# A hybrid GLA and S5 decoder block: the S5 tables loaded beside the scan and built second matrix first, the powers transposed one product later, two buffers for the attention output

## The chip, the cores and the metric

The kernel runs on one core of a Trainium2 chip. The core has five engines that run their own instruction streams in order: TensorE (PE in the profile, with its weight loads as PEld), VectorE (DVE), ScalarE (ACT), GpSimd (POOL) and SyncE (SP). SP, ACT and POOL also issue DMAs, each in the order of its own queue. The metric is the device time of one execution in microseconds; lower is better.

## The reference

What is computed, cut to what matters here: a GLA attention branch and a grouped complex-diagonal S5 branch on the same projected input, gated and added, then a squared-ReLU MLP.

```python
xn = rmsnorm(h, g_mix_pre[l]);  proj = xn @ w_in[l]      # q, k, v, r, a_low, u, z_gla, z_ssm
log_a = log_sigmoid(a_low @ w_gate_up[l] + b_gate[l]) / GATE_TAU
o = gla_chunked(q * DK**-0.5, k, v, log_a)               # 4 heads, key 128, value 256
o = rmsnorm(o, gla_norm_g[l]) * silu(r);  y_gla = o @ w_o_gla[l]
# S5: 64 groups of 16 channels, 64 complex states each
lam = exp((a_re + 1j * a_im) * dt);  bb = (lam - 1) / (a_re + 1j * a_im) * b
x_t = lam * x_{t-1} + bb @ u_t;      y_t = real(c @ x_t) + d_skip * u_t
glu = gelu(y_s) @ w_glu[l] + b_glu[l];  y_ssm = glu[:D] * sigmoid(glu[D:])
mixed = sigmoid(z_gla) * y_gla + sigmoid(z_ssm) * y_ssm
h = h + rmsnorm(mixed @ w_out[l], g_mix_post[l])
h = h + rmsnorm(square(relu(rmsnorm(h) @ w_ff1[l])) @ w_ff2[l])
```

512 tokens and 16 meta tokens, width 1024, all in float32.

## The kernel before, in words

**Products.** Activations stand with features on the partitions. Each product of 128 output features is one entry of the list `dense` and one call of `slot()`: a weight tile of 128x1024 is loaded by SP (`wraw`, line 167), ScalarE rounds it to its high half (`whi`, L161), VectorE subtracts to get the low half (`wlo`, L176), and PE runs 24 matmuls of 512 columns (eight steps of whi by xh, whi by xl, wlo by xh; `mm3`, L60 in the profile since a helper issues every matmul). Each of the three tiles has three buffers, and a slot fetches two weights ahead, so the halves of the third product on can only be made when a product has ended. The list is in this order: u3 to u7 (S5 input), four z_ssm gates and one z_gla gate, then per head v, v, k, q and a z_ssm gate, then four z_gla gates, r0 to r7 (the gate r of the attention output), and z5, o0, o1, o2, z6, o3, o4, z7, o5, o6, o7, where o is the output projection. PE keeps the order of the program; on VectorE and ScalarE a list scheduler sets the order of the instructions when the program is built, after data and buffers.

**S5.** 64 groups in eight blocks of eight. First come parameters in `chain` and `powers`: Lr and Li are the powers 0 to 8 of lam, E8 those of the normalised lam to the eighth. `lam_rows` transposes Lr and Li on PE (16 transposes of 64x64, line 65), ScalarE copies them to `lamn`, and they are written to DRAM (`lamd`, L776). `b_rows` turns the scaled input matrix (tile `bar`), `c_rows` the output matrix (tiles `cnat` and `cnatx` into CA and CB, L745). Each block then has two matrices, made by `tables` on VectorE in four pieces: the first, M1 (64 complex states by eight steps by 16 channels), from B and lam, which are loaded from DRAM by broadcast (L994, L996); the second, M2, from CA, CB, Lr and Li (L986 to L988). `turns` makes the rotations E of the block (`erot`, L236 to L239), `kernels` the impulse response from M2 (written to `kpad` and read again as M3, L1046), `scan` the states (16 matmuls of U and M1, then v, a scan, X; L1052 to L1069), `output` the result.

**The loop.** One iteration per block b has five slots. Between them stand the attention of head b (`decays`, `turn_values`, `turn_keys`, `scores`, `states`), the outputs of head b-1, and the S5 work: turns(b), the loads of block b+1, a slot, kernels(b) and output(b-1), a slot, scan(b), and then the four pieces of the tables of block b+1, one after each of the scan and the next slots. B and lam have one buffer each, and M1's pieces work on B in place.

**Attention outputs.** `outputs` ends with `on` (L960), `turn_outputs` transposes its two halves into PSUM, ScalarE scales each into `oT` (L969), and GpSimd's queue stores it (`og`, L970). A product r later reads it back (`ro`), and VectorE multiplies (L1120, L1121) and splits it (`ogl`, L1123). The four PSUM banks named `sm` serve all such transposes in rotation.

The lines that the change and the prediction's steps touch:

Of the kernel before, what the change touches and what calls it, by code (L numbers as in the profile page):

```python
# [12 lines left out]
ALU = mybir.AluOpType  # L13
# [3 lines left out]
P = 128  # L17
D = 1024
KT = D // P
SEQ = 512  # L20
# [16 lines left out]
T8 = 8  # L37
NCK = NT // T8
NST = NCK - 1
GRP = 64  # L40
NST_N = 64
HG = 16
GB = 8
NBLK = GRP // GB
# [5 lines left out]
def hybrid_block(ctx: ExitStack, tc: tile.TileContext, io, out: bass.AP):  # L50
    nc = tc.nc
    V, S, G = nc.vector, nc.scalar, nc.gpsimd
# [267 lines left out]
    V, S = InOrder(nc.vector), InOrder(nc.scalar)  # L320
# [107 lines left out]
    V, S = nc.vector, nc.scalar  # L428
# [122 lines left out]
    CA = mk(p5, [P, GRP, HG], tag="CA")  # L551
# [249 lines left out]
        pass  # L801
    slot()
    powers()
    lam_rows()
    b_rows()
    slot()
    for s_ in cr:
        pass
    sga.close()
    st5.close()  # L810

# [7 lines left out]

    kmetas = [mk(pgb, [P, P], tag=f"kmeta{i}") for i in range(2)]  # L820
    vmetas = [mk(pgb, [P, DV], tag=f"vmeta{i}") for i in range(2)]
    for t in (*kmetas, *vmetas):
        G.memset(t, 0.0)

    class Head:
# [136 lines left out]
        def turn_outputs(self):  # L962
            for v in range(2):
                m = 2 * self.h + v
                ps = bank()
                for t in range(TT):
                    PE.transpose(ps[:, t * P : (t + 1) * P], self.on[:, t, v * P : (v + 1) * P], ident)
                oT = mk(pgb, [P, SEQ], tag="oT", bufs=1)
                S.activation(oT, ps, AF.Copy, scale=vecs[:, V_GN + m : V_GN + m + 1])  # L969
                nc.gpsimd.dma_start(og_dram[m], oT)  # L970

    class Block:
# [14 lines left out]
            V.tensor_mul(ta, b_[:, gg].unsqueeze(2).to_broadcast(sh), lib)  # L987
            V.tensor_add(d, d, ta)  # L988

        def loads(self):  # L990

            self.B = mk(b5, [P, GB, 2, NST_N], tag="B")
            self.lam = mk(b5, [P, 2, GB, NST_N], tag="lam")
            nc.sync.dma_start(self.B.rearrange("p g c n -> p (g c n)"), bard[:, self.gs, :].rearrange("h g n -> h (g n)").unsqueeze(0).to_broadcast([T8, HG, GB * 2 * NST_N]))  # L994
            for i in range(2):
                nc.sync.dma_start(self.lam[:, i].rearrange("p g n -> p (g n)"), lamd[i, :, self.gs, :].rearrange("l g n -> l (g n)").unsqueeze(1).to_broadcast([T8, HG, GB * NST_N]))  # L996

        def tables(self):

            M1 = self.M1 = mk(b5, [P, GB, 2, NST_N], tag="M1", bufs=1)  # L1000
            self.M2 = mk(b5, [P, GB, 9, HG], tag="M2", bufs=2)
            B, (lr, li) = self.B, (self.lam[:, i].unsqueeze(2).to_broadcast([P, GB, 2, NST_N]) for i in range(2))
            V.tensor_mul(M1, B, lr)
            yield
            self.table(self.M2, 9, CA, CB, 0)
            yield
            V.tensor_mul(B, B, li)  # L1007
            V.tensor_sub(M1[:, :, 0], M1[:, :, 0], B[:, :, 1])
            V.tensor_add(M1[:, :, 1], M1[:, :, 1], B[:, :, 0])
            yield  # L1010
            self.table(self.M2, 9, CA, CB, 4)
            yield

        def turns(self):

            self.d0 = mk(b5, [P, GB, NST], tag="d0")
            S.copy(self.d0, prm[:, M8, self.gs].unsqueeze(2).to_broadcast([P, GB, NST]))
            G.memset(self.d0[:, :, 0:1], 0.0)
            self.E = mk(b5, [P, 2, GB, NST], tag="E")
            S.copy(self.E[:, :, :, :9], E8[:, :, self.gs, :])  # L1020
            U = self.U = mk(b5, [P, GB, NCK], tag="U", bufs=2)

            for sp in range(T8):
                nc.sync.dma_start(U[sp * HG : (sp + 1) * HG], ud[self.blk][:, :, T8 - 1 - sp, :].rearrange("g h c -> h g c"))
            for n in (8, 16, 32):
                erot(self.E, n, n, b5)
# [14 lines left out]
        def scan(self):  # L1041

            M3 = self.M3 = mk(b5, [P, GB, P], tag="M3", bufs=1)
            for sp in range(T8):
                s = T8 - 1 - sp
                nc.sync.dma_start(M3[sp * HG : (sp + 1) * HG], kpad[self.gs].rearrange("g h l -> h g l")[:, :, 112 - 16 * s : 240 - 16 * s])  # L1046
            U, E = self.U, self.E
            v, vs = (mk(b5, [P, GB, NST], tag=t, bufs=1) for t in ("v", "vs"))

            def turn(src, gg):  # L1050

                V.tensor_mul(vs[:64, gg], src[64:], E[64:, 1, gg])  # L1052
                V.tensor_mul(vs[64:, gg], src[:64], E[:64, 1, gg])  # L1053

            for g0 in range(0, GB, 4):
                ps = bank()
                pv = ps[:, : 4 * NST].rearrange("p (g c) -> p g c", g=4)
                for g in range(4):
                    PE.matmul(pv[:, g], self.M1[:, g0 + g].rearrange("p c n -> p (c n)"), U[:, g0 + g, :NST], start=True, stop=True)
                gg = slice(g0, g0 + 4)  # L1060
                V.tensor_mul(v[:, gg], pv, E[:, 0, gg])
                turn(pv, gg)
            V.tensor_sub(v, v, vs)
            flat = v.rearrange("p g c -> p (g c)")
            V.tensor_tensor_scan(flat, self.d0.rearrange("p g c -> p (g c)"), flat, 0.0, op0=ALU.mult, op1=ALU.add)  # L1065
            X = self.X = mk(b5, [P, GB, NST], tag="X", bufs=1)
            V.tensor_mul(X, v, E[:, 0])
            turn(v, slice(0, GB))
            V.tensor_add(X, X, vs)  # L1069
# [80 lines left out]
    for kind, m in (("z", 5), ("o", 0), ("o", 1), ("o", 2), ("z", 6), ("o", 3), ("o", 4), ("z", 7), ("o", 5), ("o", 6), ("o", 7)):  # L1150
        if kind == "o":
            o_slot(m)
        else:
            gate_slot(C_ZG, m, zg)
    blocks[0].loads()
    first = blocks[0].tables()
    for _ in range(4):
        next(first, None)
# [1 line left out]
    for b, blk in enumerate(blocks):  # L1160
        this = heads[b] if b < HEADS else None
        last = heads[b - 1] if 0 < b <= HEADS else None
        blk.turns()
        following = iter(())
        if b + 1 < NBLK:
            blocks[b + 1].loads()
            following = blocks[b + 1].tables()
        slot()
        blk.kernels()
        if b:  # L1170
            blocks[b - 1].output()
        if this:
            this.decays()
        slot()
        blk.scan()
        if last:
            last.outputs()
        if this:
            this.query_decay()
        next(following, None)  # L1180
        slot()
        if this:
            this.turn_values()
        next(following, None)
        slot()
        if this:
            this.turn_keys()
        if last:
            last.turn_outputs()
        if b == HEADS:  # L1190
            sgb.close()
            sg.close()
            so = ExitStack()
            po_ = pool("po", stack=so, padded=True)
            ogh = mk(po_, [P, KT, SEQ], F32R, tag="ogh")
            ogl = mk(po_, [P, KT, SEQ], F32R, tag="ogl")
        next(following, None)
        slot()
        if this:
            this.scores()  # L1200
            this.states()
        if b:
            blocks[b - 1].turn_output()
        next(following, None)
# [347 lines left out]
```

## Time and profile before

| | |
|---|---|
| median of three runs | 918.82 us (918.14 to 924.5) |
| the profiled execution | 919.62 us, its span 917.9 us |
| granted TensorE clock, mean | 0.989 |
| busy: PE, DVE, ACT, POOL | 889.4, 668.6, 402.4, 91.0 us |
| HBM | 191 GB/s over the span |

How to read it: the span runs from the first to the last instruction of one execution. A timeline row gives start and length in us, engine, line, operation, tile written and tiles read, and in brackets the idle time of the engine ahead of it with what ended it. A row of the waits gives who waited for whom: us in total, times, the longest. A row of the windows gives a stretch, its length, then busy us and number of instructions of PE, PEld, DVE, ACT and POOL, the granted clock, the busy share of the DMA engines and GB/s. A row of groups gives busy us, mean ns, idle time. SPq rows are the issue of a DMA on SP's queue, with waiting for room in it. Rows with a start, a length and no idle bracket that name only engine and line come from the chain that ended last.

### The profile page before, as it was taken

The page shows a single profiled execution, that of the slowest core. Times are in us where ns is not written, and L with a number is a line of the kernel's source. Part 1 is how long each engine was busy: PE and PEld are TensorE (multiplying, and loading weights), DVE is VectorE, ACT ScalarE, POOL GpSimd, SP SyncE. Part 2 cuts the span into 40 slices and gives each one's busy share as a digit, 9 for nine tenths or more (in the row PEclk, how much of TensorE's full clock was granted, in tenths as well). Part 3 has the DMA queues.
Part 4 walks back from the last instruction along what each step waited for, and adds up shares of the span by engine and source line. Part 5 has one row for each costly group of instructions (what it writes and reads, how often), then busy time and mean ns, then how long its engine had stood idle before and what let it go on. Part 6 is the DMA issues. An engine that isn't in the chain of part 4 may idle for free.

```text
span 917.9 us, 13370 instructions
## 1 busy us (share of the span) xinstructions
PE 889.4 (97%) x4924; PEld 755.2 (82%) x4924; DVE 668.6 (73%) x1182; ACT 402.4 (44%) x656; POOL 91.0 (10%) x169
## 2 busy tenths in 40 slices
PE   8998999999999999699999999999999999999996
PEld 6997898889898788588888888988888888888885
DVE  7896968959696879936644566576766668688786
ACT  6362353655653343312433454332332226666663
POOL 1221100010202011021200000011111100000001
PEclk9998999999999999999999999999999999999999
DMA  7745756373746575547854683359898976966664
GB/s 230 204 117 174 173 143 147 82 192 84 184 92 185 130 210 130 150 130 223 279 161 140 178 237 102 138 179 344 291 332 294 347 250 206 302 203 188 182 207 139
DMA packets 175588, 176.13 MB, mean 192 GB/s; under 512 B 22637, under 2 KB 137393, under 8 KB 175522
## 3 DMA queue, kind: packets, MB, share of 16 engines
q1 hardware_dynamic: 159280, 118.94, 47.0%
q0 software_dynamic: 15072, 52.39, 16.4%
q10 hardware_dynamic: 1170, 3.94, 1.2%
q8 instruction: 39, 0.64, 0.3%
q14 instruction: 27, 0.22, 0.1%
HBM read 139.81 MB, written 35.42 MB: 191 GB/s over the span
## 4 chain that ended last, share of the span: by engine, by line
PE 80%; DVE 7%; issue 5%; DMA 4%; ACT 2%; SPq 1%; DVEq 0%; POOL 0%; ACTq 0%; POOLq 0%
PE mm L60 59%; PE sm L60 19%; PE sm L65 2%; DMA wraw<-in_w_in_dram 1%; DMA b<-bd 1%; DMA og<-oT 1%; DVE wlo L176 1%; DMA xt<-in_x_dram 0%; DVE vs L1052 0%; DVE v L1065 0%; PE mm L65 0%; DVE B L1007 0%; SPq L1046 0%; DVE b L484 0%; DVE vs L1053 0%
## 5 line engine op out<-in xcount | busy, mean ns | idle before, releaser
L161 ACT ACTIVATE whi<-wraw 128x1024 fp32r<-128x1024 f32 x101 | 106.8, 1059 | 223.7 <-PE mm L60 196.0
L176 DVE TENSOR_TENSOR wlo<-wraw,whi 128x1024 fp32r<-128x1024 f32 x101 | 123.2, 1221 | 86.6 <-ACT whi L161 86.6
L60 PE MATMUL mm<-xh,whi 128*128 128x512 f32 (+2 forms) x544 | 184.6, 339 | 0.5 <-ACT xh L78 0.5
L60 PE MATMUL mm<-xh,wlo 128*128 128x512 f32 (+2 forms) x544 | 180.8, 332 | 3.7 <-DVE wlo L176 3.6
L60 PE MATMUL mm<-xl,whi 128*128 128x512 f32 (+2 forms) x544 | 180.5, 332 | 0.7 <-DVE xl L78 0.7
L60 PEld LDWEIGHTS mm<-xh,wlo 128*128 128x128 f32 x544 | 104.2, 192 | 13.8 <-DVE wlo L176 4.0
L60 PEld LDWEIGHTS mm<-xh,whi 128*128 128x128 f32 x544 | 104.3, 192 | 11.8 <-issue 1.0
L60 PEld LDWEIGHTS mm<-xl,whi 128*128 128x128 f32 x544 | 104.2, 192 | 9.6 <-DVE xl L78 1.1
L60 PE MATMUL mm<-hh,whi 128*128 128x512 f32 (+1 forms) x280 | 104.0, 371 | 0.0
L60 PE MATMUL mm<-hl,whi 128*128 128x512 f32 (+1 forms) x280 | 103.8, 371 | 0.0
L60 PE MATMUL mm<-hh,wlo 128*128 128x512 f32 (+1 forms) x280 | 103.8, 371 | 0.0
L1429 DVE TENSOR_TENSOR wlo<-wraw,whi 128x1024 fp32r<-128x1024 f32 x56 | 68.4, 1223 | 21.0 <-ACT whi L1425 20.9
L60 PE MATMUL sm<-wlo,fh 128*128 128x512 f32 x192 | 74.8, 390 | 0.0
L60 PE MATMUL sm<-whi,fh 128*128 128x512 f32 x192 | 74.7, 389 | 0.0
L60 PE MATMUL sm<-whi,fl 128*128 128x512 f32 x192 | 74.7, 389 | 0.0
L1425 ACT ACTIVATE whi<-wraw 128x1024 fp32r<-128x1024 f32 x56 | 58.7, 1049 | 18.3 <-PE mm L60 11.7
L60 PEld LDWEIGHTS mm<-hh,whi 128*128 128x128 f32 x280 | 52.8, 188 | 9.1
L60 PEld LDWEIGHTS mm<-hh,wlo 128*128 128x128 f32 x280 | 52.7, 188 | 9.1
L60 PEld LDWEIGHTS mm<-hl,whi 128*128 128x128 f32 x280 | 52.8, 188 | 8.9
L60 PE MATMUL mm<-gh,whi 128*128 128x512 f32 x128 | 49.8, 389 | 0.0
L60 PE MATMUL mm<-gl,whi 128*128 128x512 f32 x128 | 49.8, 389 | 0.0
L60 PE MATMUL mm<-gh,wlo 128*128 128x512 f32 x128 | 49.8, 389 | 0.0
(422 smaller groups left out, 1589.2 us busy)
## 6 DMA issues: line engine op xcount, KB each, us to landing
wraw<-in_w_ff_dram SPq DMA_DIRECT2D x56, 512.0 KB
wraw<-in_w_in_dram SPq DMA_DIRECT2D x48, 512.0 KB
w2raw<-in_w_ff_dram POOLq DMA_DIRECT2D x16, 1024.0 KB, 8.7
t2d<-w2t POOLq DMA_DIRECT2D x16, 1024.0 KB, 5.9
wraw<-t2d SPq DMA_DIRECT2D x32, 512.0 KB
wraw<-in_w_glu_dram SPq DMA_DIRECT2D x16, 512.0 KB
B<-bard SPq DMA_DIRECT2D x8, 512.0 KB
lam<-lamd SPq DMA_DIRECT2D x16, 256.0 KB
```

The source lines that it names most:

```text
L60: ins = nc.tensor.matmul(*args, **kw)
L65: ins = nc.tensor.transpose(*args, **kw)
L161: S.activation(dst, src, AF.Copy, scale=scale)
L176: V.tensor_sub(lo, raw, f32(hi))
L1425: halved = S.activation(bh, raw, AF.Copy)
L1429: V.tensor_sub(bl, raw, f32(bh))
```

## The change

Five edits:

1. `lam_rows()` is called behind the next slot and behind the rest of `c_rows`, not right behind `powers()`.
2. `loads` of block b+1 is called behind `scan(b)`, not behind `turns(b)`. The loads of block 0 are issued by GpSimd's queue, the others by SP's as before.
3. `tables` makes both pieces of M2 first and then both pieces of M1.
4. `oT` has two buffers.
5. `d0`, the factor of the scan, is one tile for all blocks, filled with zeros once; each block's copy writes all but its first column, and the eight small fills of that column are gone.

```diff
@@ preparation
     slot()
     powers()
-    lam_rows()
     b_rows()
     slot()
     for s_ in cr:
         pass
+    lam_rows()
...
-    for t in (*kmetas, *vmetas):
+    d0 = mk(b5, [P, GB, NST], tag="d0")
+    for t in (*kmetas, *vmetas, d0):
         G.memset(t, 0.0)
@@ turn_outputs
-                oT = mk(pgb, [P, SEQ], tag="oT", bufs=1)
+                oT = mk(pgb, [P, SEQ], tag="oT", bufs=2)
@@ loads
-        def loads(self):
+        def loads(self, queue=nc.sync):
...
-            nc.sync.dma_start(self.B...)
+            queue.dma_start(self.B...)
             for i in range(2):
-                nc.sync.dma_start(self.lam...)
+                queue.dma_start(self.lam...)
@@ tables
+            for g0 in (0, 4):
+                self.table(self.M2, 9, CA, CB, g0)
+                yield
             V.tensor_mul(M1, B, lr)
-            yield
-            self.table(self.M2, 9, CA, CB, 0)
             yield
             V.tensor_mul(B, B, li)
             V.tensor_sub(M1[:, :, 0], M1[:, :, 0], B[:, :, 1])
             V.tensor_add(M1[:, :, 1], M1[:, :, 1], B[:, :, 0])
             yield
-            self.table(self.M2, 9, CA, CB, 4)
-            yield
@@ turns
-            self.d0 = mk(b5, [P, GB, NST], tag="d0")
-            S.copy(self.d0, prm[:, M8, self.gs].unsqueeze(2).to_broadcast([P, GB, NST]))
-            G.memset(self.d0[:, :, 0:1], 0.0)
+            S.copy(d0[:, :, 1:], prm[:, M8, self.gs].unsqueeze(2).to_broadcast([P, GB, NST - 1]))
@@ the loop
-    blocks[0].loads()
+    blocks[0].loads(nc.gpsimd)
...
         if b + 1 < NBLK:
-            blocks[b + 1].loads()
             following = blocks[b + 1].tables()
...
         blk.scan()
+        if b + 1 < NBLK:
+            blocks[b + 1].loads()
```

How the order of instructions moves, at three places. First TensorE in the preparation, before. The product of mm_1039 is u7, that of whi_928 the first z_ssm gate; Lr and Li are the powers, bar the B rows:

```order
L60 MATMUL mm_1039<-xh_98,wlo_846 128x272
L65 MATMUL sm_1123<-ident_79,Lr_484 64x64 x8
L65 MATMUL sm_1133<-ident_79,Li_485 64x64 x8
L65 MATMUL sm_1144<-ident_79,bar_522 128x64 x8
L65 MATMUL sm_1154<-ident_79,bar_522 128x64 x8
L60 MATMUL mm_1170<-xh_98,whi_928 128x512
```

And now, where whi_1008 is the second z_ssm gate:

```order
L60 MATMUL mm_1149<-xh_98,wlo_930 128x512
L65 MATMUL sm_1177<-ident_79,cnat_510 128x128 x4
L65 MATMUL sm_1183<-ident_79,cnatx_511 128x128 x4
L65 MATMUL sm_1189<-ident_79,cnat_510 128x128 x4
L65 MATMUL sm_1195<-ident_79,cnatx_511 128x128 x4
L65 MATMUL sm_1201<-ident_79,Lr_484 64x64 x8
L65 MATMUL sm_1211<-ident_79,Li_485 64x64 x8
L60 MATMUL mm_1260<-xh_98,whi_1008 128x512
```

The transposes of the powers moved behind one whole product and the C rows; nothing else on TensorE changes its place.

Second, SP's queue in the iteration of block 1, before. U is the input of block 2, B and lam its tables, b the decay sums of head 2, wraw the weights:

```order
L1024 DMA U_1825<-ud_103 16x8x66 x6
L994 DMA B_1852<-bard_498 128x1x1024
L996 DMA lam_1853<-lamd_499 128x1x512 x2
L167 DMA wraw_1857<-in_w_in_dram 128x8x128
L856 DMA b_339_1953<-bd_481 128x528
L167 DMA wraw_1974<-in_w_in_dram 128x8x128
```

And now:

```order
L1022 DMA U_1823<-ud_103 16x8x66 x6
L167 DMA wraw_1850<-in_w_in_dram 128x8x128
L857 DMA b_336_1946<-bd_481 128x528
L167 DMA wraw_1967<-in_w_in_dram 128x8x128
L995 DMA B_2060<-bard_498 128x1x1024
L997 DMA lam_2061<-lamd_499 128x1x512 x2
L167 DMA wraw_2110<-in_w_in_dram 128x8x128
```

The three table loads moved behind two weight tiles and b.

Third, VectorE in the iteration of block 6, before. v, vs and X are scan(6), M_758 and B_4081 the first matrix of block 7, M_759 its second:

```order
L1063 TENSOR_TENSOR v_4210<-v_4210,vs_4211 128x520
L1003 TENSOR_TENSOR M_758_4235<-B_4081,lam_4082 128x1024
L1065 SCALAR_TENSOR_TENSOR v_4210<-d_724_4049,v_4210 128x520
L1007 TENSOR_TENSOR B_4081<-B_4081,lam_4082 128x1024
L1067 TENSOR_TENSOR X_4230<-v_4210,E_4052 128x520
L1052 TENSOR_TENSOR vs_4211<-v_4210,E_4052 64x520
L1053 TENSOR_TENSOR vs_4211<-v_4210,E_4052 64x520
L1008 TENSOR_TENSOR M_758_4235<-M_758_4235,B_4081 128x8x64
L1069 TENSOR_TENSOR X_4230<-X_4230,vs_4211 128x520
L1009 TENSOR_TENSOR M_758_4235<-M_758_4235,B_4081 128x8x64
L988 TENSOR_TENSOR M_759_4236<-M_759_4236,mta_4359 128x576
L237 TENSOR_TENSOR epb_4378<-E_4366 128x128
```

After eleven more rows of E follows the low weight half of product o1 (wlo_4242). Now E is made right behind X, and its last rows and what follows are:

```order
L236 TENSOR_TENSOR mta_4375<-E_4352 128x512
L237 TENSOR_TENSOR epb_4376<-E_4352 128x512
L238 TENSOR_TENSOR E_4352<-mta_4375,epb_4376 128x8x32
L239 TENSOR_TENSOR E_4352<-mta_4375,epb_4376 128x8x32
L1007 TENSOR_TENSOR M_752_4223<-B_4218,lam_4219 128x1024
L1009 TENSOR_TENSOR B_4218<-B_4218,lam_4219 128x1024
L1010 TENSOR_TENSOR M_752_4223<-M_752_4223,B_4218 128x8x64
L1011 TENSOR_TENSOR M_752_4223<-M_752_4223,B_4218 128x8x64
L176 TENSOR_TENSOR wlo_4233<-wraw_4229,whi_4231 128x1024
```

The first matrix of block 7 moved from among the rows of the scan to behind E, right ahead of the low half of o1. (The changed kernel's lines 1007 to 1011 are the lines 1003 to 1009 of before.)

More of the change, by code (lines that the diff above doesn't have):

```diff
@@ L988, in table @@
             V.tensor_add(d, d, ta)
-        def loads(self):
+        def loads(self, queue=nc.sync):
             self.B = mk(b5, [P, GB, 2, NST_N], tag="B")
             self.lam = mk(b5, [P, 2, GB, NST_N], tag="lam")
-            nc.sync.dma_start(self.B.rearrange("p g c n -> p (g c n)"), bard[:, self.gs, :].rearrange("h g n -> h (g n)").unsqueeze(0).to_broadcast([T8, HG, GB * 2 * NST_N]))
+            queue.dma_start(self.B.rearrange("p g c n -> p (g c n)"), bard[:, self.gs, :].rearrange("h g n -> h (g n)").unsqueeze(0).to_broadcast([T8, HG, GB * 2 * NST_N]))
             for i in range(2):
-                nc.sync.dma_start(self.lam[:, i].rearrange("p g n -> p (g n)"), lamd[i, :, self.gs, :].rearrange("l g n -> l (g n)").unsqueeze(1).to_broadcast([T8, HG, GB * NST_N]))
+                queue.dma_start(self.lam[:, i].rearrange("p g n -> p (g n)"), lamd[i, :, self.gs, :].rearrange("l g n -> l (g n)").unsqueeze(1).to_broadcast([T8, HG, GB * NST_N]))
         def tables(self):
@@ L1064, in scan @@
             flat = v.rearrange("p g c -> p (g c)")
-            V.tensor_tensor_scan(flat, self.d0.rearrange("p g c -> p (g c)"), flat, 0.0, op0=ALU.mult, op1=ALU.add)
+            V.tensor_tensor_scan(flat, d0.rearrange("p g c -> p (g c)"), flat, 0.0, op0=ALU.mult, op1=ALU.add)
             X = self.X = mk(b5, [P, GB, NST], tag="X", bufs=1)
```

## The prediction

> **What bounds the kernel now.** I read the page's first part, then who waits for whom on the tensor engine, and only then the timelines around each of its waits.
>
> ```profile
> PE 889.4 (97%) x4924; PEld 755.2 (82%) x4924; DVE 668.6 (73%) x1182; ACT 402.4 (44%) x656; POOL 91.0 (10%) x169
> PE mm L60 <- DVE wlo L176: 8.1, 2, 4.5
> PE sm L65 <- DVE Lr L222: 4.1, 3, 2.1
> PE sm L65 <- ACT oT L969: 2.7, 2, 1.9
> PE sm L65 <- ACT on L960: 1.5, 2, 0.9
> PE sm L65 <- DVE Li L227: 0.4, 1, 0.4
> ```
>
> TensorE (PE) is the bound: it is busy for 97% of the span of 917.9 us. The change alters neither the number nor the size of a matmul, so it can win only what PE loses in waits and what the clock loses after them. The waits that matter (each row: total us, how often, the longest) sum to 16.8 us. Three kinds are touched: the powers Lr and Li (4.5 us), the output copies oT and on (4.2 us), and two waits for the low weight half wlo (8.1 us). I take them in order of time.
>
> **Part 1: the powers turned one product on.** Before, the eight transposes of Lr follow the product that ends at 74.28, and VectorE is still computing those powers.
>
> ```profile
> 74.28 0.34 PE L65 MATMUL sm<-ident,Lr 64*64 64x64 f32 x2
> 81.02 1.91 PE L65 MATMUL sm<-ident,bar 64*128 64x64 f32 x16
> 82.93 7.21 PE mm L60 x24
> 84.00:86.00 2.00, 2.00 (x6) 1.53 (x5) 0.00 (x0) 0.07 (x1) 0.00 (x0) 0.50 0.93 197
> 90.14 1.75 PE sm L65 x16
> 91.64 0.48 PE L60 MATMUL mm<-xh,whi 128*128 128x512 f32 x1
> 283.50 5.47 PE mm L60 x24
> 67.62 0.65 PE L65 MATMUL sm<-ident,nat 64*128 64x64 f32 x7
> 83.25 0.41 DVE L239 TENSOR_TENSOR E<-mta,epb 128x256 f32<-128x256 f32 x1
> 90.61 0.75 DVE L745 TENSOR_SCALAR CA<-sm,sgn 128x512 f32<-128x512 f32 x1 [6.96 <-PE sm L65]
> ```
>
> From 74.28 to 91.64, where the next product begins, PE took 17.36 us. In it are the waits, the turned B rows (1.91), a product of 24 matmuls that took 7.21 us where one at full clock takes 5.47 (the windows row gives a granted clock of 0.50 at 84 to 86 us), and the 16 turned C rows (1.75). After the change PE goes from 74.28 straight to the B rows (16 at the rate of the nat row, 7 in 0.65, is 1.5 us), the product (5.47, both weight halves are ready) and the C rows (1.75): 83.0. Then come the powers. Their two PSUM banks (four rotate) are those of the first two C groups, so VectorE has to empty these first. It ends its own chain at 83.25 + 0.41 and needs at most 0.75 for each of the two copies: the second is done at 85.1, and eight transposes behind it (0.7 by the nat row) end at 85.8. A wait of about 1 us stays. The next product begins at 85.8 instead of 91.64: **5.8 us won**. Bounds: 7 if the banks do not hold it, 4.5 if the clock still falls after that wait (the 1.3 us of part 2).
>
> What is late next is lamn, the turned powers on their way through DRAM, now needed by block 0's first matrix.
>
> ```profile
> 82.14 0.86 POOL L776 DMA_DIRECT2D lamd<-lamn  x1 [5.64 <-ACT lamn L775]
> 85.84 1.22 SPq L996 DMA_DIRECT2D lam<-lamd  x2
> w2raw<-in_w_ff_dram POOLq DMA_DIRECT2D x16, 1024.0 KB, 8.7
> 113.50 0.28 PE L60 MATMUL mm<-xh,whi 128*128 128x256 f32 x1
> ```
>
> The lam loads stood until 85.84, 3.7 us after the store at 82.14. Now the store goes out near 86.3, lam near 90.0, from GpSimd's queue, where only the stores of sigmoid tiles are queued behind it; nobody waits soon for those. B and lam together are 1 MB; by the slow w2raw row they land by 99. By then VectorE has made the second matrix, which now comes first, and wants them from about 95 on. Of what is queued behind them on VectorE, PE needs first the low weight half for the product at 113.50, then at 107.7; that split stands right behind the matrix's first multiply, and the two (some 1.2 us each) are done by 101.5. So lam can be 6 us later still before PE waits, and I cost this at nothing; without that cover each us it is late is one lost.
>
> **Part 2: two buffers for oT.**
>
> ```profile
> 193.99 0.69 ACT L969 ACTIVATE oT<-sm,vecs 128x512 f32<-128x512 f32 x1 [8.15 <-DMA og<-oT]
> 194.73 0.66 PE L65 MATMUL sm<-ident,qt 128*128 128x128 f32 x4 [1.90 <-ACT oT L969]
> 195.38 7.37 PE mm L60 x48
> 205.25 6.07 PE mm L60 x48
> 240.01 0.66 PE L65 MATMUL sm<-ident,qt 128*128 128x128 f32 x4 [0.83 <-ACT oT L969]
> ```
>
> ScalarE stood 8.15 us for the store of the first half before it could write the second into the same buffer; the PSUM bank it held stopped PE for 1.90 us, and the 48 matmuls behind took 7.37 instead of 6.07. With a second buffer that is 1.9 + 1.3, and 0.83 in the next head: **4.0 us won**, bounds 2.7 (only the waits) and 4.5.
>
> **Part 3: loads where the scan stands.**
>
> ```profile
> 141.68 0.61 SPq L994 DMA_DIRECT2D B<-bard  x1
> 144.34 12.11 DMA b<-bd
> 156.47 0.69 DVE L866 TENSOR_TENSOR d<-b 128x512 f32<-128x512 f32 x1 [4.05 <-DMA b<-bd]
> 163.65 1.89 PE L60 MATMUL sm<-U,M 128*128 128x65 f32 x16
> 166.01 0.42 DVE L1061 TENSOR_TENSOR v<-sm,E 128x260 f32<-128x260 f32 x1
> 182.88 1.50 PE L65 MATMUL sm<-ident,on 128*128 128x128 f32 x8 [0.94 <-ACT on L960]
> ```
>
> Before, B for the next block stands in SP's queue until VectorE is done with the one buffer (141.68), and behind it stand a weight tile and b, which lands 12.11 us after its issue: VectorE idles 4.05 us. Half of the scan's matmuls were done near 164.6, yet VectorE reached v only at 166.01, and the chain behind v ends in the 0.94 us that PE waits for on. In the new order b goes ahead of B and B's buffer is long free; VectorE starts these rows up to 4 us sooner, which covers the 1.4 us it was late. I take **0.5 us**, bounds 0 and 1.5 (the whole row of on). The shared d0 saves eight short fills on an engine that is 10% busy: nothing.
>
> **Part 4: the two waits for wlo stay.** This is where I do not follow the waits table.
>
> ```profile
> 325.70 0.69 DVE L1120 TENSOR_TENSOR rs<-rs,mm 128x512 f32<-128x512 f32 x1 [7.52 <-ACT rs L1119]
> 335.08 1.89 PE L60 MATMUL sm<-U,M 128*128 128x65 f32 x16
> 336.11 0.43 DVE L1061 TENSOR_TENSOR v<-sm,E 128x260 f32<-128x260 f32 x1
> 366.88 0.75 DVE L986 TENSOR_TENSOR M<-CA,Lr 128x576 f32<-128x576 f32 x1
> 336.10:390.40 54.30, 46.28 (x246) 37.69 (x245) 53.64 (x94) 18.08 (x29) 3.22 (x7) 0.96 0.55 138
> 390.40:394.00 3.60, 3.56 (x10) 2.88 (x11) 2.85 (x3) 0.00 (x0) 0.55 (x1) 0.59 0.61 181
> 390.44 0.80 PE L60 MATMUL mm<-ogh,wlo 128*128 128x512 f32 x1 [4.47 <-DVE wlo L176]
> ```
>
> From the scan of block 5 to the weight split for product o1 VectorE is busy 53.64 of 54.30 us and PE only 46.28: here VectorE is the bound. I went through both orders of its rows between these two points. They hold the same work but for one table product, which now stands before v (0.75 in the row at 366.88). So the stretch shortens by that **0.7 us**, wherever its rows stand. The second oT buffer does let VectorE start its work on the r products earlier (the 7.52 us idle at 325.70), but at 336.11 it waits for PE's scan matmuls of 335.08 again, and the head start ends there. What moves is where PE stands still: the split for product z5 comes earlier, that for o1 behind the powers E and the first matrix of block 7. Instead of 3.6 and 4.5 us I expect about 0 and 9 in one piece. The clock behind it falls once more: the stretch from 390.40 has a granted clock of 0.59, which costs some 1.5 us. A longer wait may cost up to 1.5 us more than that; I take **0.6 lost**.
>
> By the Trainium skill, "TensorE: Matmul & The Clock Gate", Part 1, the clock is halved after an idle window of about 3.4 us and freed only after a busy one, and these windows run free of the program. An estimate from its figures is 1.7 to 3.4 us lost behind such a wait, so 0.2 to 1.9 more than now in place of my 0.6; the trace agrees in size with its 1.3 and 1.5 us.
>
> **Sum.** 5.8 + 4.0 + 0.5 + 0.7 - 0.6 = 10.4 us. The profiled execution took 919.62 (span 917.9), so 909.2; it lay 0.8 above the median of 918.82, so **908.4 us** against that median.
>
> **The rivals.**
> - The wlo waits dissolve, since the split for z5 stands earlier and the loads no longer block weights in SP's queue. For it: the 8.1 us are the largest entry of the waits table. Against it: VectorE's 53.64 busy us, of which the change removes none. It would win 8.1 and one slow stretch of 1.5 in place of the last two terms: 898.9.
> - The lead is handed back: PE runs 10 us ahead, but VectorE, full where it makes tables, cannot follow, and PE waits for on or wlo elsewhere. For it: 73% is an average over full and half-empty stretches. Against it: VectorE idled 6.96 us in the very place where part 1 wins, and 4.05 and 7.52 later, so it can move along. With half of parts 1 to 3 gone the time is 913.6.
> - Slower: the tables of block 7 now stand in SP's queue behind the eight loads of M3, and the split for o1 stands on VectorE behind the matrix made of them.
>
> ```profile
> 369.21 3.63 SPq L1046 DMA_DIRECT2D M<-kpad  x8
> 376.89 1.22 DVE L1003 TENSOR_TENSOR M<-B,lam 128x1024 f32<-128x1024 f32 x1
> ```
>
> By the times of before, the tables would be issued by 369.21 + 3.63 + 0.61 + 1.22 = 374.7. VectorE wants them some 5 us before o1's split ends (four instructions, none over 1.22), near 385. If they land like b (12.11) that is 2 us late. It decides from a landing time of 21 us on, where the 10.4 us are eaten; at twice b's 12.11 the matrix is 14 us late and the time is 922. For it: one in-order queue with two things in it that wait. Against it: no landing in these rows is that long.
>
> **How the numbers follow.** The forecast has 72%. All bounds at their best give 905.1, at their worst 912.4; since they seldom meet, its own range is 905.5 to 911.5. The first rival has 8%, the second 15%, the slower one 5%. A measurement here can tell about 1% from no change, that is 909.6 and 928.0. Of the forecast's share 52 points lie below 909.6 and 20 above: with the first rival 60% are faster, with the second 35% the same, and 5% slower. The range that holds 8 in 10 runs from 904.3 to 914.3: it takes in the second rival and leaves out the first and the last.
>
> **What would show it.** Part 1: no wait of PE for Lr before the C rows, one of about 1 us behind them, granted clock 1.00 from 70 to 90 us, the product of 91.64 near 85.8. Part 2: no row "oT waits for og", the pair of waits for oT gone. Part 3: B behind b in SP's queue, VectorE's wait for b gone. Part 4: VectorE full between the scan of block 5 and o1's split, and one PE wait for wlo of 8 to 10 us, in place of two, near 370 to 380. The prediction is wrong if that wait is under 4 us, or if PE reaches the scan of block 5 (335.08 before) less than 8 us earlier.

## The result, and the profile after

The changed kernel takes 912.10 us (median of 6 runs, 911.67 to 912.74) where the kernel before takes 918.63 (6 runs, 917.48 to 924.50) on the same chip: a ratio of 0.992, with a 95% interval of 0.9895 to 0.9946. 6.5 us were won, 10.4 were forecast; 912.1 is 3.7 above the forecast of 908.4: just outside the forecast's own range (905.5 to 911.5), inside the one given for 8 in 10 (904.3 to 914.3). The profiled execution took 912.54 us, with a span of 910.8.

The first part of the changed kernel's page:

```profile
PE 885.9 (97%) x4924; PEld 752.6 (83%) x4924; DVE 668.6 (73%) x1182; ACT 403.1 (44%) x656; POOL 92.1 (10%) x165
```

The engines are as busy as before, PE by 3.5 us less. The waits of its tensor engine that matter here (total us, how often, the longest):

```profile
PE mm L60 <- DVE wlo L176: 8.2, 2, 5.5
PE mm L60 <- ACT whi L161: 2.6, 1, 2.6
PE sm L65 <- DVE CA L745: 1.6, 1, 1.6
PE sm L65 <- ACT on L961: 0.5, 1, 0.5
```

The waits for Lr, Li and oT are gone and those for on have shrunk from 1.5 to 0.5. In their place stands one of 1.6 behind the C rows. The waits for weights have not shrunk but grown, from 8.1 to 10.7 us, and one of them is for a high half (whi), which there was none of before.

To see where the time came from, the same matmul is looked up in both timelines. The shift is after minus before; the first loads came 0.45 us later in this execution, so each shift is understated by that.

| where PE stands | before | after | shift |
|---|---|---|---|
| product of 91.64 | 91.64 | 86.03 | -5.61 |
| turned on, first head | 182.88 | 176.23 | -6.65 |
| turned qt, first head | 194.73 | 185.83 | -8.90 |
| behind the 48 matmuls | 202.69 | 192.24 | -10.45 |
| turned qt, next head | 240.01 | 228.56 | -11.45 |
| scan of block 5 | 335.08 | 323.50 | -11.58 |
| product o0 | 379.91 | 367.26 | -12.65 |
| third matmul of o1 | 390.44 | 381.65 | -8.79 |
| next turned qt | 396.92 | 389.56 | -7.36 |
| in the last product of the MLP | 844.76 | 837.43 | -7.33 |

PE wins 12.0 us up to the scan of block 5, more than the forecast (10.3 without the last two terms), and then gives back 4.2 between that scan and 396.92. The shortfall lies in this piece.

The tensor engine's rows at these places, of the changed kernel (start, duration, ..., the wait before it):

```profile
84.87 0.63 PE L65 MATMUL sm<-ident,Lr 64*64 64x64 f32 x8 [1.55 <-DVE CA L745]
86.03 0.50 PE L60 MATMUL mm<-xh,whi 128*128 128x512 f32 x1
360.82 0.80 PE L60 MATMUL mm<-xh,wlo 128*128 128x512 f32 x1 [2.66 <-DVE wlo L176]
375.42 0.50 PE L60 MATMUL mm<-ogh,whi 128*128 128x512 f32 x1 [2.56 <-ACT whi L161]
381.65 0.80 PE L60 MATMUL mm<-ogh,wlo 128*128 128x512 f32 x1 [5.49 <-DVE wlo L176]
```

z5 still waits for its low half (2.66, it was 3.6), and o1 waits twice: for the high half of its weight, and two matmuls later for the low half.

The stretch that the prediction took to be bound by VectorE, from v of block 5 to the end of o1's split, and the stretch behind it (columns: PE, PEld, DVE, ACT, POOL busy us and counts; granted clock; DMA share; GB/s):

```profile
324.54:381.60 57.06, 46.39 (x246) 37.56 (x245) 53.62 (x92) 19.20 (x29) 2.98 (x5) 0.93 0.62 147
381.60:390.00 8.40, 8.35 (x27) 6.67 (x28) 3.11 (x4) 0.00 (x0) 0.55 (x1) 0.64 0.59 187
```

VectorE is busy for 53.62 us of it, and was for 53.64: the work is the same, but the stretch is 57.06 long where it was 54.30. VectorE stands idle in it. For what, ScalarE's timeline shows, and then VectorE's own:

```profile
326.82 1.06 ACT L161 ACTIVATE whi<-wraw 128x1024 fp32r<-128x1024 f32 x1 [6.41 <-DMA wraw<-in_w_in_dram]
327.79 0.58 ACT L1117 ACTIVATE rs<-mm 128x512 f32<-128x512 f32 x1
...
374.31 1.06 ACT L161 ACTIVATE whi<-wraw 128x1024 fp32r<-128x1024 f32 x1 [2.20 <-DMA wraw<-in_w_o_gla_dram]
```

```profile
328.40 0.69 DVE L1118 TENSOR_TENSOR rs<-rs,mm 128x512 f32<-128x512 f32 x1 [2.55 <-ACT rs L1117]
...
376.65 1.22 DVE L1007 TENSOR_TENSOR M<-B,lam 128x1024 f32<-128x1024 f32 x1
380.38 1.22 DVE L176 TENSOR_TENSOR wlo<-wraw,whi 128x1024 fp32r<-128x1024 f32 x1
```

ScalarE stands 6.41 us for the weight of product r5. Behind it in ScalarE's order is the sigmoid of product r2, and for that VectorE waits 2.55 us. At 374.31 ScalarE has waited again, for o1's weight; its low half is made only at 380.38, behind the matrix of block 7. SP's queue tells why these weights are late:

```profile
312.06 0.61 SPq L995 DMA_DIRECT2D B<-bard  x1
312.72 1.19 SPq L997 DMA_DIRECT2D lam<-lamd  x2
313.96 0.46 SPq L167 DMA_DIRECT2D wraw<-in_w_in_dram  x1
...
356.99 3.63 SPq L1044 DMA_DIRECT2D M<-kpad  x8
360.72 0.60 SPq L995 DMA_DIRECT2D B<-bard  x1
361.36 1.20 SPq L997 DMA_DIRECT2D lam<-lamd  x2
362.66 2.73 SPq L167 DMA_DIRECT2D wraw<-in_w_o_gla_dram  x2
```

r5's weight is issued right behind the 1 MB of tables for block 6 and is there 12.9 us later (313.96 to 326.82). o1's weight (the first of the two at 362.66) stands behind the eight M3 loads of block 6, which wait for that block's kernel rows, and behind the 1 MB for block 7. Only the 1 MB is new: in the kernel before, o1's weight stood behind the M3 loads too (they began at 369.21, in the prediction's lines):

```profile
372.94 1.02 SPq L167 DMA_DIRECT2D wraw<-in_w_o_gla_dram  x2
```

### The profile page after: what moved, and what is told of

Same layout as the page of the kernel before. It is cut to its first block, busy times and chain, and to the rows that moved or that the text cites. A ratio compares the mean times of both kernels' runs of the same rounds, so it can differ in the third digit from the quotient of the medians.

```text
span 910.8 us, 13359 instructions
## 1 busy us (share of the span) xinstructions
PE 885.9 (97%) x4924; PEld 752.6 (83%) x4924; DVE 668.6 (73%) x1182; ACT 403.1 (44%) x656; POOL 92.1 (10%) x165
## 4 chain that ended last, share of the span: by engine, by line
PE 85%; DVE 9%; DMA 2%; issue 2%; ACT 2%; SPq 0%; DVEq 0%; ACTq 0%
PE mm L60 62%; PE sm L60 20%; PE sm L65 2%; DMA wraw<-in_w_in_dram 1%; DVE wlo L176 1%; DVE mta L236 1%; DVE rs L1119 0%; DVE vs L1050 0%; DVE epb L237 0%; DVE vs L1051 0%; DVE v L1063 0%; DVE b L484 0%; PE mm L65 0%; DVE ogl L1121 0%; DVE mn L482 0%
## 5 line engine op out<-in xcount | busy, mean ns | idle before, releaser
L1424 ACT ACTIVATE whi<-wraw 128x1024 fp32r<-128x1024 f32 x56 | 58.7, 1049 | 18.5 <-PE mm L60 11.7
```

The lines of the kernel that those rows point to most:

```text
L1424: halved = S.activation(bh, raw, AF.Copy)
```

## The experiments

**The parts one by one.** Four kernels on one chip, beside 11 runs of the kernel before (median 918.88 us). My theory was that the wins add up and part 3 makes the loss; its rival, that the lead is handed back whoever makes it.

Part 1 alone:

```diff
     powers()
-    lam_rows()
     b_rows()
 ...
         pass
+    lam_rows()
     sga.close()
```

> The kernel before with part 1 of the change alone (the powers turned one product on). Theory (the three wins add up; the loss of some 4 us between the scan of block 5 and the split for product o1 comes from part 3, the loads): the product of 91.64 near 86, the lead of about 6.0 us kept to the end since the loads stand where they were: 6.0 won, 912.7 us. Rival (the loss belongs to the lead itself: whoever reaches the scan of block 5 earlier finds VectorE no further on and pays it back): 6 us ahead at that scan, but only 2 to 4 at the end, 914.5 to 916.5.

Measured: 912.42 us (911.13 to 915.63), ratio 0.9928 [0.9911, 0.9944]. The number is the one expected, the way to it is not: the product of 91.64 comes 6.1 us sooner; 1.6 are lost to the clock behind the C rows; and at the first head's end 3.6 us are won that I had booked for part 2, because the wait for oT is not there although there is one buffer. In the stretch behind the scan of block 5 nothing is lost (shift -8.53 at 369.15, the first matmul behind the scan of block 6, and -8.55 at 396.92; this profiled execution began 1.25 us early, so only the difference of the two counts).

Part 2 alone:

```diff
-                oT = mk(pgb, [P, SEQ], tag="oT", bufs=1)
+                oT = mk(pgb, [P, SEQ], tag="oT", bufs=2)
```

> The kernel before with part 2 alone (two buffers for oT). Theory: 3.6 us at the first head's end (1.9 waited, 1.3 to 1.5 of clock) and 1.0 in the next head, all of it kept: 4.6 won, 914.1 us. Rival (the lead is paid back in the stretch that VectorE fills): 0 to 2 won, 916.5 to 918.7.

Measured: 915.13 us (914.61 to 916.43), ratio 0.9956 [0.9942, 0.9969]: 3.75 won. The waits for oT go as forecast, but the wait for on just before grows from 0.94 to 1.84 and in the profiled execution the clock falls behind it. In the last stretch 0.3 is lost, so the lead is kept.

Part 3 alone, the core of its diff (block 0's loads on GpSimd's queue and the shared d0 are with it):

```diff
         blk.turns()
 ...
-            blocks[b + 1].loads()
             following = blocks[b + 1].tables()
 ...
         blk.scan()
+        if b + 1 < NBLK:
+            blocks[b + 1].loads()
```

> The kernel before with part 3 alone (loads beside the scan, second matrix first, block 0's loads on GpSimd's queue, shared d0). Theory: the wait for on goes (1.3 won), then the loads of block 6 stand ahead of r5's weight and those of block 7 ahead of o1's: VectorE's stretch is 2.8 us longer and the clock behind o1's wait costs 1.4 more; 2.9 lost, 921.5 us. Rival (part 3 is harmless and the lead is what is paid back): 1.3 won or nothing, 917.3 to 918.6.

Measured: 915.03 us (913.85 to 916.73), ratio 0.9955 [0.9941, 0.997]: 3.85 won, and both numbers expected were wrong. The loss is there as the theory has it (shift -5.43 at 369.15, -3.21 at 396.92), but so are 4.6 us won at the ends of the first two heads, again with one oT buffer.

Parts 1 and 2 without part 3:

> Parts 1 and 2 without part 3: the loads, the tables and d0 as in the kernel before. Theory: 6.0 and 4.6 won and neither the 1.3 of part 3 nor its 4.2 of loss: 10.6 won, 908.0 us, the split for o1 still 54 us behind v of block 5, with two waits for wlo as before. Rival (the lead is paid back whoever makes it): 10.6 ahead at the scan of block 5 and 6 to 7 at the end, 911.5 to 912.5, like the changed kernel.

Measured: 912.16 us (910.18 to 913.45), ratio 0.9916 [0.9899, 0.9933]. The rival's number, but not by its mechanism: in the last stretch 1.3 are lost, with the clock low from 382 to 390 us, not the 4.2 of the changed kernel. The wins themselves do not add up. Alone the three parts win 6.5, 3.75 and 3.85, together 14.1; the changed kernel wins 6.5. So two things had to be found out: what the second oT buffer is still worth, and what makes the loss of part 3.

**What the wait for oT was.** One buffer again in the changed kernel:

```diff
-                oT = mk(pgb, [P, SEQ], tag="oT", bufs=2)
+                oT = mk(pgb, [P, SEQ], tag="oT", bufs=1)
```

> The changed kernel with one oT buffer again (parts 1 and 3 without part 2). Theory formed from the four runs before (the wait for oT was made by B and lam moving beside the og store; parts 1 and 3 each take them away from it, and the store then lands before PE needs the bank): no wait of PE for oT at the first head's end, and the time of the changed kernel, 912.1 within 1. Rival (the prediction's own part 2: the second buffer is worth 3.6 and 1.0 there): 4.6 slower, 916.7 us.

Measured: 910.36 us (909.68 to 912.28), ratio to the kernel before 0.9906 [0.9885, 0.9926]. That is 1.7 less than the changed kernel took on its chip, where at most 1 was expected; the two intervals overlap. So no gain of the second buffer is left once the other parts are there. ScalarE's second oT of the first head, with one buffer and parts 1 and 3:

```profile
185.55 0.69 ACT L970 ACTIVATE oT<-sm,vecs 128x512 f32<-128x512 f32 x1 [5.87 <-DMA og<-oT]
```

It still waits for the store, but 5.87 us (5.93 with part 1 alone, 5.46 with part 3 alone) and not 8.15, and PE does not wait for the bank. In the kernel before, 1 MB of tables is issued from 181.10 to 182.94, 2.3 us ahead of the store at 185.19; with part 1 alone its last issue ends at 172.68 and the store goes out at 180.10. That the tables delay the store is read from these rows; no run takes the tables away there, so it is not shown beyond that. One row speaks against it as the whole cause: in the second head with part 1 alone the last issue ends 6.2 us ahead of the store, and ScalarE still waits 7.25 us.

**What makes the loss.** The loads of B and lam of all blocks in GpSimd's queue, and nothing else changed:

```diff
         if b + 1 < NBLK:
-            blocks[b + 1].loads()
+            blocks[b + 1].loads(nc.gpsimd)
```

> The changed kernel with the loads of B and lam of all blocks issued from GpSimd's queue. Theory (the order in SP's queue makes the loss: r5's weight stands behind 1 MB for block 6, o1's behind 1 MB for block 7): r5's weight lands some 6 us earlier, VectorE's 2.55 us idle behind v of block 5 and PE's 2.56 us for o1's high half go; 2.6 to 4.4 won, 908 to 909.5 us. Rival (the DMA engines are full there, 0.88 to 1.06 between 316 and 327 us, so the weight shares them whatever the queue): within 1 of 912.1.

Measured: 903.83 us (900.76 to 904.77), ratio to the kernel before 0.9823 [0.9799, 0.9848]: 8.3 us better than the changed kernel, about twice what the theory gave. The product r5 first. Its tables and its weight:

```profile
301.99 0.62 POOL L995 DMA_DIRECT2D B<-bard  x1 [1.67 <-DVE E L239]
313.32 0.40 SPq L167 DMA_DIRECT2D wraw<-in_w_in_dram  x1
```

B of block 6 goes out at 301.99, released by VectorE (lam, two loads, from 295.92); in SP's queue it went out at 312.06. So the megabyte is over 10 us ahead of r5's weight, which lands 4.6 us after its issue and not 12.9, and VectorE does not stand idle for it.

Then o1: SP's queue in this kernel, ScalarE's row for its weight, VectorE's rows for o1's split and the matrix of block 7, and the stretch (columns as above):

```profile
343.51 0.39 SPq L167 DMA_DIRECT2D wraw<-in_w_o_gla_dram  x1
347.04 0.41 SPq L167 DMA_DIRECT2D wraw<-in_w_o_gla_dram  x1
359.09 3.64 SPq L1044 DMA_DIRECT2D M<-kpad  x8
```

```profile
358.56 1.06 ACT L161 ACTIVATE whi<-wraw 128x1024 fp32r<-128x1024 f32 x1 [0.72 <-DMA wraw<-in_w_o_gla_dram]
```

```profile
364.56 1.22 DVE L176 TENSOR_TENSOR wlo<-wraw,whi 128x1024 fp32r<-128x1024 f32 x1
371.59 1.22 DVE L1007 TENSOR_TENSOR M<-B,lam 128x1024 f32<-128x1024 f32 x1
```

```profile
325.70:381.60 55.90, 55.90 (x306) 45.96 (x308) 55.21 (x93) 18.86 (x30) 8.41 (x14) 1.00 0.64 164
```

o1's weight (the second o weight, 347.04) now goes out ahead of the M3 loads, 15.6 us earlier than at 362.66. Its split, at 364.56, stands ahead of the matrix of block 7 (371.59) and not behind it (376.65 and 380.38). The landing is no shorter: 11.5 us, beside the tables of block 7 in the other queue (344.49 to 348.76), where the changed kernel had 11.7 (362.66 to 374.31). What is won is the earlier issue. VectorE is as full as before, 55.21 of 55.90 us in a stretch of much the same rows, and yet PE is busy for all of the 55.90 at clock 1.00: no wait for z5, none for o1. So it was not how much VectorE has to do, but which row stands ahead of the split. That order, like the place of o1's weight in SP's queue, is made when the program is built; why both came out otherwise here is not shown. The rival's time falls; its sharing of the DMA engines is seen in the 11.5 us of o1's weight, which comes early enough to bear it. The gain is more than the 4.2 given back: the waits of 3.58 for z5 and 4.47 for o1, which the kernel before had, are gone too. One wait for a low half stays, 2.58 us at 394.57, for product o3.

Two more kernels on another chip (kernel before: 919.28 us) move the loads of one block each, to part the two late weights:

```diff
-            blocks[b + 1].loads()
+            blocks[b + 1].loads(nc.gpsimd if b + 1 == 6 else nc.sync)
```

> The changed kernel with the loads of B and lam of block 6 alone on GpSimd's queue. In SP's queue r5's weight is then ahead by 1 MB, but o1's weight still stands behind the eight M3 loads of block 6 and the lam loads of block 7. Theory (two losses with two causes: r5's weight behind the tables of block 6, 2.6 us of VectorE; o1's weight behind M3 and the tables of block 7, 8 us of PE and its clock): VectorE's 2.55 us idle goes, z5's wait of 2.66 goes, but o1's waits stay or grow to 8 to 11: 909.5 to 912. Rival (the first of the two sets both): 904 to 906.

Measured: 908.00 us (907.02 to 909.01), ratio 0.9868 [0.9843, 0.9893]. VectorE's idle time and z5's wait are gone, o1's waits stay:

```profile
370.38 0.50 PE L60 MATMUL mm<-ogh,whi 128*128 128x512 f32 x1 [0.66 <-ACT whi L161]
378.28 0.79 PE L60 MATMUL mm<-ogh,wlo 128*128 128x512 f32 x1 [7.16 <-DVE wlo L176]
```

They are 0.66 and 7.16, in sum 7.8 where the changed kernel has 8.05. It is 1.5 us better than the expectation, which had left out the clock: with z5's wait went the low clock behind it (0.58 and 0.57 from 360 to 364 us in the changed kernel; here it does not fall there).

The same for block 7 alone (b + 1 == 7):

> The changed kernel with the loads of B and lam of block 7 alone on GpSimd's queue. SP's queue then has o1's weight directly behind the M3 loads, still not ahead of them; r5's weight stays behind the tables of block 6. Theory: PE's 2.56 us for o1's high half go, the wait for its low half shrinks by at most the 1.8 us of two issues and what the landing gains: 908 to 910.5. Rival (block 7's loads make the whole wait for o1): 904 to 906. Rival (M3's place makes it all): 912.

Measured: 910.95 us (909.94 to 911.99), ratio 0.9902 [0.9874, 0.9929]: 1.2 better than the changed kernel, a little less than expected, and by the intervals not clear of it. z5's wait is there as before (2.79), those for o1 are 1.29 and 3.29, in sum 4.6. So the waits say that block 7's tables make part of o1's wait; the M3 loads that its weight still stands behind are left. The two kernels win 4.1 and 1.2, together 5.3 of the 8.3: only with both blocks' loads out of SP's queue does o1's weight go out ahead of M3.

**Is VectorE the bound at all?** Two kernels on the chip of the one-buffer run (kernel before: 918.49 us) take work from VectorE:

```diff
             for g0 in (0, 4):
-                self.table(self.M2, 9, CA, CB, g0)
+                if self.blk < 7:
+                    self.table(self.M2, 9, CA, CB, g0)
+                else:
+                    G.memset(self.M2[:, g0 : g0 + 4], 0.0)
                 yield
```

> The changed kernel with the second matrix of block 7 left out (its table is filled with zeros on GpSimd, so the output of that block is another): six instructions of 0.75 us, 4.1 us of VectorE in a row, taken out of the stretch before the split for z5. Theory (VectorE sets that stretch): the wait of 2.66 us for z5 goes and the split for o1 ends 4.1 us earlier, 4 won, 908 us. Rival (o1's split is set by the landing of its weight and of block 7's tables): z5's wait goes, o1's grows by as much, 912.1.

Measured: 908.41 us (907.73 to 909.31), ratio 0.9883 [0.9863, 0.9903], 3.7 better than the changed kernel. That is the theory's number, but the trace gives half of it to the rival. z5's wait is gone, and the low clock behind it. The waits for o1 are still 5.9 (whi) and 1.8 (wlo), as ScalarE's row says:

```profile
374.00 1.06 ACT L161 ACTIVATE whi<-wraw 128x1024 fp32r<-128x1024 f32 x1 [5.43 <-DMA wraw<-in_w_o_gla_dram]
```

o1's weight is there at 374.00, and at 374.31 in the changed kernel, however early VectorE is done. In this kernel VectorE's work no longer holds z5, and the landing of the weight makes 5.9 of the 7.7 us for o1. In the changed kernel the landing is not all: there the split comes 6 us after it, behind E and the matrix.

```diff
-            V.tensor_sub(ogl[:, m], sg_, f32(ogh)[:, m])
+            G.tensor_sub(ogl[:, m], sg_, f32(ogh)[:, m])
```

> The changed kernel with the eight subtractions that make the low half of the r products (0.69 us each on VectorE, six of them behind v of block 5) on GpSimd. Theory (VectorE sets that stretch, GpSimd is 10% busy): 0.6 times 6 is 3.6 us less on VectorE, the waits for z5 and o1 together 3.6 shorter, 908.5 us. Rival (GpSimd's work slows VectorE's beside it, or comes late): no gain, 912 or more.

Measured: 911.23 us (910.74 to 912.00), ratio 0.9913 [0.9894, 0.9933]: 0.9 better than the changed kernel and by the intervals not clear of it, where 3.6 was expected. ScalarE still waits 6.72 us for r5's weight, and PE 2.10 and 2.76 for z5, 0.86 and 4.49 for o1, 10.2 in all where the changed kernel has 10.7. A subtraction takes 1.46 us on GpSimd (median of the eight), 0.69 on VectorE. Taking this work off the full engine hardly helps while the weight is late.

**Place or queue, and a better kernel.** Parts 1 and 2, with the loads in the place of the kernel before, but in GpSimd's queue:

```diff
-            blocks[b + 1].loads()
+            blocks[b + 1].loads(nc.gpsimd)
         slot()
         blk.kernels()
```

> Parts 1 and 2 with the loads where the kernel before has them (behind the turns, old order of the tables) but on GpSimd's queue. SP's order has o1's weight ahead of M3, as in the changed kernel with all loads on GpSimd's queue. Theory (which queue the loads are in decides, not their place): within 2.5 of that one's 903.8, so 903 to 906.5, no wait of PE for wlo of z5 or o1. Rival (the place beside the scan is needed too): 908 or more.

Measured: 903.11 us (902.77 to 904.83), ratio 0.982 [0.9793, 0.9847]. The place of the loads and the order of the tables decide nothing that can be measured; the queue of the loads does: 9 us between this kernel and parts 1 and 2 with the loads in SP's queue (912.16). PE does not wait for z5 or o1, only 0.63 us for o2 and 2.61 for o3. Even the wait for on is 0.5 here, as with part 3.

Last, the wait for CA that part 1 left:

```diff
     for s_ in cr:
         pass
+    slot()
     lam_rows()
 ...
-    for _ in range(4):
+    for i in range(4):
         next(first, None)
-        slot()
+        if i:
+            slot()
 ...
-            blocks[b + 1].loads()
+            blocks[b + 1].loads(nc.gpsimd)
```

> The changed kernel with all loads on GpSimd's queue and the powers turned one more product on, behind the first z_gla product, so that VectorE has emptied the C rows' banks long before. Theory: PE's wait of 1.55 us for CA goes and the 3.4 us at half clock behind it (1.6 us) in nearly all runs: 903.8 - 3.1 = 900.7 us. Rival (lamd comes 5.5 us later, block 0's first matrix and the split behind it too, and PE waits for that split): 903 to 906.

Measured: 900.13 us (899.05 to 900.65), ratio to the kernel before 0.9779 [0.9752, 0.9805]. It beats both kernels, by some 19 and 12 us. The waits of its tensor engine:

```profile
PE mm L60 <- DVE wlo L176: 2.6, 1, 2.6
PE sm L60 <- DMA grow<-in_g_mix_pre_dram: 2.5, 1, 2.5
PE mm L60 <- DVE xl L78: 0.7, 2, 0.3
PE sm L65 <- ACT on L962: 0.5, 1, 0.5
```

The wait for CA is gone. lam lands later, and VectorE waits 2.23 us for it ahead of block 0's first matrix, but the split behind that is done at 106.4, in time for its product; no new wait of PE has come. What is left in the middle is the one of 2.6 for wlo of o3, near 390 us, behind the scan of block 7.

## Why the prediction was right in its sign and 3.7 us off

- **Part 1** (5.8 us): right, with its working. Corrected for the late start it won 6.1, and the wait that it left behind the C rows is 1.55 where "about 1" was said. The lam loads were there at 99.77 (99 was said) and the split behind them was done at 102.1 (101.5 was said), in time. The fall of the clock behind that wait stood in its bounds alone; in this profiled execution it did not come, in those of seven of the nine other kernels with this wait it did (last section).
- **Part 2** (4.0 us): the size came near (3.8 and 1.0 at the ends of the two heads, 4.8 in all, just over its upper bound of 4.5), but in part by luck, for the cause was another. The step "with a second buffer that is 1.9 + 1.3, and 0.83 in the next head" holds in the kernel before (3.75 won by the buffer alone), but each of parts 1 and 3 alone takes PE's wait at the first head away too, and the buffer adds nothing to them (910.36 with one, 912.10 with two). I took the 8.15 us for the store as the store's own length; with the tables further ahead of it, it is 5.5 to 5.9 in this head.
- **Part 3** (0.5 us, bounds 0 and 1.5): where it was looked for it won 1.0 (the shift goes from -5.61 to -6.65): the first head's wait for on is gone, a later one of 0.5 stays. Its price was booked nowhere: I followed what the new place frees in SP's queue (b ahead of B) and not what it now stands in front of. The weights of r5 and o1 are what stands there.
- **Part 4** (0.7 won, 0.6 lost): here the prediction failed, at the step "they hold the same work but for one table product ... so the stretch shortens by that 0.7 us, wherever its rows stand". The table product did leave the stretch, but VectorE's busy time stayed at 53.62 (53.64 before), and the stretch grew by 2.8, of which 2.55 is VectorE waiting, by way of ScalarE, for r5's weight. A full engine was taken for a bound; but in the kernel with all loads in GpSimd's queue VectorE is busy for 55.21 of 55.90 us with much the same rows, and PE does not wait once. The clock term was 0.6 and measured 1.4: from o1's third matmul to the next turned qt PE took 7.91 us, before 6.48. Together the two terms should have given +0.1 and gave -4.2; the wins up to that point were 1.7 larger than forecast (12.0 for 10.3), which leaves an error of 2.6 in the profiled execution; by the medians it is 3.7, and the 1.1 between lies within what executions of one kernel differ by.
- **The waits**: "about 0 and 9 in one piece" was 2.66 for z5 and 2.56 + 5.49 for o1, parted by two matmuls. The condition for being wrong, a wait under 4 us, was not met, but the reason for the wait was another.
- **The rivals**: the one with a lead handed back came nearest in time (913.6), but the lead is not handed back as such: parts 1 and 2, each alone, keep theirs through this stretch (0.0 and 0.3 lost), and together they lose 1.3 of it. The first rival, in which the waits for wlo dissolve, was put aside because the change removes none of VectorE's work; once the loads leave SP's queue, both waits do dissolve, with the work still there, and the time comes down to 903.8, on the way to the 898.9 given for it. The slower rival named the right place, block 7's loads behind M3 in one in-order queue; it looked at the tables, which come in time, and not at the weight issued behind them.

## What to carry to other kernels

When a load is moved in an in-order queue, list not only what it is now behind but what is now behind it, and follow the first weight there to the engine that splits it and to whatever that engine has in line. An engine that is 99% busy ahead of a wait is only the bound if all that work must come before the row that is waited for; ask when that row's own inputs land. And wins read off one trace are not independent: a wait for a buffer, a store and the load beside it can be one and the same time, and three parts that win 6.5, 3.8 and 3.9 us alone may win 6.5 together.

## What the runs showed of the hardware

**One and the same wait may or may not cost clock.** Behind the C rows PE waits 1.54 to 1.58 us in ten of the kernels. In the profiled executions of seven of these the granted clock falls behind it, in three (the changed kernel and the two with one block's loads moved) it does not. Two of them, the stretches of the changed kernel and then of the kernel with part 1 alone:

```profile
84.00:86.00 2.00, 1.13 (x16) 0.95 (x16) 2.00 (x4) 0.82 (x2) 0.54 (x1) 1.00 0.56 145
86.00:88.00 2.00, 2.00 (x11) 1.61 (x10) 2.00 (x4) 0.70 (x2) 0.98 (x2) 1.00 0.73 253
```

```profile
84.00:86.00 2.00, 2.00 (x12) 1.62 (x10) 2.00 (x3) 1.03 (x2) 0.66 (x1) 0.61 0.88 299
86.00:88.00 2.00, 2.00 (x6) 1.54 (x6) 0.80 (x2) 0.00 (x0) 1.06 (x5) 0.54 0.63 106
```

The low stretch lasts some 3.4 us (the two windows of 2 us lost 0.39 and 0.46 of their clock, 1.7 us in all, which at half clock is 3.4 us). It costs 1.6: from the turned Lr to the scan of block 0 PE takes 37.19 us with part 1 alone and 35.63 in the changed kernel. The wait for on does the same: 1.74 us with part 1 alone and no fall, 1.75 with parts 1 and 2 and a fall to 0.59 and 0.56. The row with part 1 alone, then the row and the stretches behind it with parts 1 and 2:

```profile
178.02 1.50 PE L65 MATMUL sm<-ident,on 128*128 128x128 f32 x8 [1.74 <-ACT on L960]
```

```profile
178.72 1.50 PE L65 MATMUL sm<-ident,on 128*128 128x128 f32 x8 [1.75 <-ACT on L960]
```

```profile
180.00:182.00 2.00, 2.00 (x8) 1.57 (x7) 1.87 (x8) 1.98 (x3) 1.08 (x2) 0.59 1.09 187
182.00:184.00 2.00, 2.00 (x7) 1.57 (x6) 1.95 (x4) 0.39 (x1) 0.00 (x0) 0.56 1.17 312
```

So a wait of 1.5 to 1.8 us is priced with 1.6 us of clock times a chance, not with a fixed sum, and one profiled execution does not tell it. The Trainium skill, "TensorE: Matmul & The Clock Gate", Part 1, has the clock judged in windows of about 3.4 us that run free of the program; the length of these falls, and that the same wait has one or not, agree with that. It puts the fall behind a whole idle window; here a wait of less than half of one was enough in seven executions of ten.

**A weight behind a megabyte.** A 512 KB weight issued right behind 1 MB of broadcast tables in SP's queue was there 12.9 and 11.7 us after its issue (r5's and o1's in the changed kernel). With the tables in GpSimd's queue the two part: r5's weight landed in 4.6 us, the tables having gone out 10 us ahead of it, and o1's, with the tables issued within 3 us of it, in 11.5 us. Beside a megabyte of tables such a weight thus landed 7 to 8 us later in either queue; other loads moved there too, so the tables' own share is not shown. What the other queue won in these runs is the time of issue: r5's tables and o1's weight went out sooner.
